# GLU weights requested ahead of the state-space tables, tables requested as buffers come free, decays filled on the spot, input products cut into pieces of 32 states

## The chip, the cores and the metric

The kernel runs on one core of a Trainium2 chip. A core has TensorE (PE, matmul, writes to PSUM), VectorE (DVE), ScalarE (ACT), GpSimd (POOL) and SyncE (SP, which here only queues DMA transfers). Each engine takes its instructions in its own order; between engines there are semaphores. The metric is the device time of one execution in microseconds (us), as the median of several runs.

## The reference

Four pre-norm residual layers over 256 tokens of 1024 features, all in float32. The mixers are stick-breaking attention, a chunked gMLP, a state-space layer ("S5"), and attention again; after each of them comes a convolution-gated MLP ("FFN"). Only the S5 mixer is touched:

```
u  = (xn @ w_in).reshape(B, L, 64 groups, 16)
bu = einsum('gph,blgh->blgp', bbar, u)               # complex, 64 states a group
x_t = a * x_{t-1} + bu_t                             # complex diagonal recurrence
y  = Re(einsum('ghp,blgp->blgh', c, x)) + d_skip * u
a, g = split(gelu(y) @ w_glu);   out = a * sigmoid(g)   # w_glu: 1024 x 2048
```

## The kernel before

**Phases.** The eight phases (attention, FFN, gMLP, FFN, S5, FFN, attention, FFN) run one behind the other, tokens in two blocks of 128. A matmul with weights is three matmuls of split operands: a weight chunk of 128x2048 values is loaded ("raw", 1 MB), and ACT makes its rounded part `wh` (L73) and DVE the rest `wl` (L74), each in two halves of 128x1024.

**One list of weight chunks.** The class `Weights` goes through the chunks of all phases in order. `dma_to(i)` requests raw chunks up to i from SP, `prep_to(i)` converts up to i, `take()` hands out the next. There are three raw buffers and six `wh`/`wl` pairs. S5 has in this list four input chunks (ssin 0 to 3), five tables (gt0, p0, bb, gt1, p1) and eight GLU chunks, called G0 to G7 here. A table is not converted: it is loaded straight into a `wh`/`wl` pair (L56) from DRAM, where GpSimd's DMA queue stored it earlier. gt holds the input matrices, p the output matrices of 16 pairs of groups, bb the input matrices in another layout. `dma_to` stops at a table that has not been reached yet (L35 to L37).

**S5 in the time domain.** 256 tokens are 64 steps of 4. `ucopy(h)` (L1247 on ACT, L1245 on DVE) brings u into place; `gmm(i)` (L1159) makes the input products of a quarter i (8 of 32 pairs of groups) in PSUM, 16 matmuls of a 128x128 weight; each streams 112 columns, of which the following matmul overwrites all but 64. `scan(i)` (L1169 to L1190) rotates the products (four products, a difference on GpSimd, a sum), runs the real recurrence of the two parts (L1178) with the decay table `mg`, and rotates back into the states X(i) with four products on DVE and two sums on GpSimd (L1187, L1190). The rotation factors are the tables t0 (quarter 0) and T (quarters 1 to 3). `kmm(n)` (L1199), `kd(n)` (L1204) and `kevac(n)` (L1211, 16 copies on ACT) make the kernel kk(n) inside a step. `ymm(i, parts)` (L1224) sums the output of quarter i from kk and X in pieces of 32 rows, `yevac(i)` (L1232, L1235, L1236) applies the gelu and splits it, and `glu(c)` multiplies by a chunk of w_glu. `gate` (L1310 to L1312) joins the halves.

**What sets the order.** Nothing is planned at run time: each engine runs in the order of the Python calls, and SP issues transfers in that order, waiting for a buffer where one is not free yet. So a transfer can't pass one that was queued ahead of it. In ACT's and DVE's order the conversion of G0 stands between the first `ucopy` and the second, hence ahead of scan(0). The decay table `mg` is computed by GpSimd during an earlier FFN, stored to DRAM (L1067) and loaded into one of the three raw buffers (L1110), which it holds until scan(3) has read it.

Of the kernel before, what the change touches and what calls it, by code (L numbers as in the profile page):

```python
# [8 lines left out]
F32 = mybir.dt.float32  # L9
# [12 lines left out]
class Weights:  # L22
# [10 lines left out]
    def dma_to(self, i):  # L33
        while self.nd < min(i, len(self.srcs)):
            if self.srcs[self.nd][1] == "tab":  # L35
                if self.npz <= self.nd:
                    return  # L37
                self.nd += 1
                continue
            t = self.raw_p.tile([128, 2048], F32, tag="raw", name=f"raw{self.nd}")  # L40
            for s in (slice(0, 1024), slice(1024, 2048)) if self.nd == 0 else (slice(0, 2048),):
                self.nc.sync.dma_start(t[:, s], self.srcs[self.nd][0][:, s])
            self.raw[self.nd] = t
            self.nd += 1
# [691 lines left out]
class S5(Phase):  # L736
    def __init__(self, k, i, g):
        super().__init__(k, i, g)
        self.done = 0
        d = k.dram  # L740
        self.d_gt = d.tile([128, 2, 2, 2048], F32, name="d_gt")
        self.d_p = d.tile([128, 2, 2, 2048], F32, name="d_p")
        self.d_b = d.tile([128, 2048], F32, name="d_b")
        self.d_w = d.tile([8, 2, 32, 64], F32, name="d_w")
        self.d_t = [d.tile([128, 2048], F32, name=f"t{r}") for r in range(2)]
        self.d_s = d.tile([128, 1024], F32, name="d_s")
        self.d_m = d.tile([128, 2048], F32, name="mg")
        self.par = k.const.tile([128, 19, 32], F32, name="spar")

    def sources(self):  # L750
# [299 lines left out]
    def tables_c(self, pool):  # L1050
        nc = self.nc
        self.own = pool.tile([128, 4], F32, tag="own", bufs=1, name="own")
        nc.sync.dma_start(self.own[:, :], self.k.ins["own"])
        yield from self.tables_t(pool)
        yield from self.tables_p(pool)
        yield from self.tables_m(pool)

    def tables_m(self, pool):
        nc, k = self.nc, self.k
        P = self.par  # L1060
        for h in range(2):
            ps = slice(16 * h, 16 * h + 16)
            m = pool.tile([128, 16, 64], F32, tag="full", bufs=1, name="m")
            nc.gpsimd.tensor_copy(m[:, :, :], P[:, 0, ps].unsqueeze(2).to_broadcast([128, 16, 64]))
            nc.gpsimd.memset(m[:, :, 0:1], 0.0)
            yield
            nc.gpsimd.dma_start(self.d_m[:, 1024 * h:1024 * h + 1024], m[:, :, :].rearrange("p a c -> p (a c)"))  # L1067

    def tables_t(self, pool):

# [33 lines left out]
    def head(self, b, mid):  # L1104
        FFN.head(self, b, mid)
        if b == 0:
            k, w = self.k, self.k.w
            w.prep_to(w.use + 3)
            self.mg = w.raw_p.tile([128, 2048], F32, tag="raw", name="mg")
            self.nc.sync.dma_start(self.mg[:, :], self.d_m[:, :])  # L1110
            self.t0 = k.big.tile([128, D], F32, tag="gb", name="t0")
            for r in range(2):
                self.nc.sync.dma_start(self.t0[:, 512 * r:512 * r + 512], self.d_t[r][:, 0:512])

    def body(self):
        k, nc, w = self.k, self.nc, self.k.w
# [3 lines left out]
        for m in range(3):  # L1120
            FFN.transposes(self, m, k.bank(4 + m))
        k.proj_feat(n, k.bank(7), 1)
        tabs = [w.take() for _ in range(3)]
        TT = []
        for i, tag in enumerate(("xth", "xtl")):
            t = k.big.tile([128, 2048], F32, tag=tag, name=f"T{i}")
            TT.append(t)

        def load_t(c):
            for i in range(2):  # L1130
                nc.sync.dma_start(TT[i][:, c], self.d_t[i][:, c.start + 512:c.stop + 512])

        load_t(slice(0, 512))
        tabs += [w.take() for _ in range(2)]
        load_t(slice(512, 1536))
        gt0, p0, bb, gt1, p1 = (w.hl[t] for t in tabs)
        self.kk.append(bb[1][:, :].rearrange("p (a j c) -> p a j c", a=16, j=4))
        nc.gpsimd.memset(bb[1][:, :], 0.0)
# [4 lines left out]
        MG = self.mg[:, :].rearrange("p (a c) -> p a c", a=32)  # L1143
# [6 lines left out]
        def wide(flat, o, a):  # L1150
            return flat[:, o:min(o + 112, flat.shape[1], o + 512 - 64 * a)]

        def gmm(i):
            for a in range(8):
                pr = 8 * i + a
                u = wide(U[pr // 16].rearrange("p a c -> p (a c)"), 64 * (pr % 16), a)
                for r in range(2):
                    o = gb(i, r)[:, 64 * a:64 * a + u.shape[1]]
                    nc.tensor.matmul(o, GT[r][pr // 16][:, pr % 16, :], u, start=True, stop=True, skip_group_check=True)  # L1159

        def scan(i, mid=lambda: None):
            ps = slice(8 * i, 8 * i + 8)
# [6 lines left out]
            V(out=A(0), in0=b[0], in1=T[0], op=mul)  # L1169
            V(out=A(1), in0=b[1], in1=T[1], op=mul)  # L1170
            G(out=A(0), in0=A(0), in1=A(1), op=sub)
            V(out=A(2), in0=b[1], in1=T[0], op=mul)
            V(out=A(3), in0=b[0], in1=T[1], op=mul)
            mid()
            V(out=A(2), in0=A(2), in1=A(3), op=add)
            fl = lambda v: v.rearrange("p a c -> p (a c)")
            for s in (2, 0):
                nc.vector.tensor_tensor_scan(fl(A(s + 1)), fl(MG[:, ps]), fl(A(s)), 0.0, mul, add)  # L1178
            x = X[i] = [self.tmp.tile([128, 8, 64], F32, tag=f"x{r}", bufs=2, name=f"x{r}") for r in range(2)]
            lo, hi = slice(0, 63), slice(1, 64)  # L1180
            z = [t[1][:, :, lo], t[3][:, :, lo]]
# [2 lines left out]
                nc.gpsimd.memset(x[r][:, :, 0:1], 0.0)  # L1184
            V(out=t[0][:, :, lo], in0=z[0], in1=tr, op=mul)
            V(out=t[2][:, :, lo], in0=z[1], in1=ti, op=mul)
            G(out=x[0][:, :, hi], in0=t[0][:, :, lo], in1=t[2][:, :, lo], op=add)  # L1187
            V(out=x[1][:, :, hi], in0=z[0], in1=ti, op=mul)
            V(out=t[3][:, :, lo], in0=z[1], in1=tr, op=mul)
            G(out=x[1][:, :, hi], in0=t[3][:, :, lo], in1=x[1][:, :, hi], op=sub)  # L1190
# [63 lines left out]
        w.prep_to(w.use + 1)  # L1254
        ucopy(1, False)
        kmm(0)
        kmm(1)
        gmm(1)

        def lags():  # L1260
            for n in range(2):
                kd(n)
                kevac(n)

        scan(0, lags)
        gmm(2)
        ymm(0, K_)
        scan(1)
        ymm(0, X_)
        yevac(0)  # L1270
        gmm(3)
        ymm(1, K_ + X_)
        scan(2)
        yevac(1)
        ymm(2, K_)
        w.prep_to(w.use + 2)
        scan(3)
        acc = [(k.bank(0), k.bank(1)), (k.bank(3), k.bank(4))]
        self.glu(0, w.take(), acc, (0, 1))
        ymm(2, X_)  # L1280
        yevac(2)
        w.prep_to(w.use + 2)
# [119 lines left out]
```

## Time and profile before

| | |
|---|---|
| median of three runs | 1232.25 us (1228.05 to 1233.34) |
| profiled execution, its own time | 1229.2 us |
| span of its instructions | 1227.4 us, 1.8 us less |
| PE busy, weight loads busy | 97%, 89% of the span |
| DVE, ACT, POOL busy | 73%, 58%, 14% |
| mean granted TensorE clock | 0.987 |
| DMA | 239.54 MB, mean 195 GB/s |

The strips of the page cut the span into 40 slices. PE shows 9 (90% and more) in nearly all of them; the lowest digits apart from the first, 6 and 8, stand in slices 21 and 22, which is where S5's body lies (about 612 to 705 us). The timeline lists instructions in order of time: start, duration, engine, line, operation, output from inputs, tile, and in brackets the idle time of the engine and what ended it. "x64" means that so many records were merged. A matmul on float32 operands that are not split shows two records. The chain of waits follows the end of a stretch back from each instruction to what released it.

### The profile page before, as it was taken

The numbers are of one execution on the slowest core, as the hardware profiler recorded it, in microseconds if no ns is written. First come the engines' busy times: TensorE is split into PE (matmuls) and PEld (weight loads), VectorE is DVE, ScalarE is ACT, GpSimd is POOL, SyncE is SP. The second block draws the span as 40 slices with busy tenths as digits, with TensorE's granted clock in tenths as the row PEclk, the third lists the DMA queues.
The fourth block names the chain that finished last, engine by engine and source line by source line (L and its number), as shares of the span: only waits on it lengthen the run. The fifth ranks groups of instructions, "written<-read, shape, count | busy, mean of one in ns | idle before, by whom it ended". The sixth has DMA issues, their size and how long they took to land.

```text
span 1227.4 us, 21740 instructions
## 1 busy us (share of the span) xinstructions
PE 1191.1 (97%) x8944; PEld 1092.2 (89%) x8944; DVE 893.1 (73%) x1268; ACT 706.4 (58%) x1068; POOL 173.2 (14%) x314
## 2 busy tenths in 40 slices
PE   8999999999999999999968799999999999999997
PEld 5898999999897999998957699999988988999996
DVE  5665599789767699899339858866756665886673
ACT  6665576567554565667336546655545655665551
POOL 3885000000384000001103000000000000000000
PEclk9999999999999999999979899999999999999999
DMA  8533457877655266587571635655445332565530
GB/s 298 214 111 113 174 199 269 272 257 276 220 214 202 111 251 221 211 301 273 224 291 36 253 113 206 241 176 201 172 155 206 128 131 106 200 230 189 206 121 35
DMA packets 49988, 239.54 MB, mean 195 GB/s; under 512 B 14944, under 2 KB 15840, under 8 KB 24544
## 3 DMA queue, kind: packets, MB, share of 16 engines
q1 hardware_dynamic: 46352, 224.78, 50.9%
q0 software_dynamic: 3392, 13.11, 2.7%
q8 instruction: 70, 1.15, 0.4%
q14 instruction: 30, 0.25, 0.1%
q10 hardware_dynamic: 144, 0.26, 0.1%
HBM read 223.84 MB, written 14.29 MB: 194 GB/s over the span
## 4 chain that ended last, share of the span: by engine, by line
PE 89%; DVE 5%; DMA 2%; ACT 2%; issue 1%; SPq 0%; POOL 0%; DVEq 0%; POOLq 0%; ACTq 0%
PE pst L126 15%; PE pst L128 15%; PE pst L127 15%; PE pst L134 13%; PE pst L136 13%; PE pst L135 13%; DMA raw<-in_glu_dram 2%; PE pst L536 1%; DVE wl L74 1%; PE pst L181 1%; PE pst L512 1%; PE pst L553 1%; DVE wl L70 1%; DVE t L1178 1%; DMA x<-in_x_dram 1%
## 5 line engine op out<-in xcount | busy, mean ns | idle before, releaser
L74 DVE TENSOR_TENSOR wl<-raw,wh 128x1024 fp32r<-128x1024 f32 x344 | 417.4, 1238 | 75.8 <-ACT wh L73 75.8
L126 PE MATMUL pst<-xth,wh 128*128 128x256 f32 x1552 | 441.0, 284 | 0.0
L127 PE MATMUL pst<-xtl,wh 128*128 128x256 f32 x1552 | 439.2, 283 | 0.0
L128 PE MATMUL pst<-xth,wl 128*128 128x256 f32 x1552 | 439.1, 283 | 0.0
L73 ACT ACTIVATE wh<-raw 128x1024 fp32r<-128x1024 f32 x344 | 350.5, 1049 | 29.8 <-DMA raw<-in_glu_dram 22.7
L126 PEld LDWEIGHTS pst<-xth,wh 128*128 128x128 f32 x1552 | 297.7, 192 | 2.3
L127 PEld LDWEIGHTS pst<-xtl,wh 128*128 128x128 f32 x1552 | 297.8, 192 | 1.2
L128 PEld LDWEIGHTS pst<-xth,wl 128*128 128x128 f32 x1552 | 297.8, 192 | 0.0
L410 DVE SCALAR_TENSOR_TENSOR y<-pst,cw,y 128x255 f32<-128x255 f32 x352 | 160.7, 479 | 72.8 <-ACT y L406 66.6
L134 PE MATMUL pst<-wh,gh 128*128 128x512 f32 x512 | 202.3, 395 | 5.2 <-DVE gate L1311 2.5
L135 PE MATMUL pst<-wl,gh 128*128 128x512 f32 x512 | 200.5, 392 | 0.0
L136 PE MATMUL pst<-wh,gl 128*128 128x512 f32 x512 | 200.1, 391 | 0.0
L406 ACT ACTIVATE y<-pst,cw 128x256 f32<-128x256 f32 x176 | 88.1, 557 | 69.4 <-PE pst L128 64.8
L134 PEld LDWEIGHTS pst<-wh,gh 128*128 128x128 f32 x512 | 96.8, 189 | 25.6 <-DVE gate L1311 2.9
L136 PEld LDWEIGHTS pst<-wh,gl 128*128 128x128 f32 x512 | 96.6, 189 | 21.0 <-DVE gl L690 0.4
L135 PEld LDWEIGHTS pst<-wl,gh 128*128 128x128 f32 x512 | 96.7, 189 | 18.3
L134 PE MATMUL pst<-wh,xth 128*128 128x256 f32 (+1 forms) x336 | 105.9, 315 | 0.0
L135 PE MATMUL pst<-wl,xth 128*128 128x256 f32 (+1 forms) x336 | 105.4, 314 | 0.1
L136 PE MATMUL pst<-wh,xtl 128*128 128x256 f32 (+1 forms) x336 | 105.4, 314 | 0.1
L165 POOL TENSOR_TENSOR r<-m,mhalf 128x1 f32<-128x1 f32 x20 | 11.1, 554 | 666.4 <-DVE m L163 657.9
L416 ACT ACTIVATE y<-y 128x256 f32<-128x256 f32 x88 | 36.4, 419 | 75.5 <-DVE y L410 75.2
L200 ACT ACTIVATE gh<-y 128x256 fp32r<-128x256 f32 x88 | 36.1, 418 | 75.0 <-DVE y L417 75.0
(180 smaller groups left out, 1240.6 us busy)
## 6 DMA issues: line engine op xcount, KB each, us to landing
raw<-in_up_dram SPq DMA_DIRECT2D x88, 1024.0 KB, 4.9
raw<-in_down_dram SPq DMA_DIRECT2D x44, 1024.0 KB, 4.9
raw<-in_wqk_dram SPq DMA_DIRECT2D x16, 1024.0 KB, 5.0
raw<-in_wo_dram SPq DMA_DIRECT2D x8, 1024.0 KB, 4.8
raw<-in_glu_dram SPq DMA_DIRECT2D x8, 1024.0 KB, 4.9
raw<-in_wv_dram SPq DMA_DIRECT2D x7, 1024.0 KB, 4.9
gb<-in_g_dram SPq DMA_DIRECT2D x9, 512.0 KB, 5.7
d_gt<-gf POOLq DMA_DIRECT2D x4, 1024.0 KB, 7.7
```

What stands on the lines that cost most here:

```text
L73: nc.scalar.activation(h[:, s], r[:, s], AF.Copy)
L74: nc.vector.tensor_tensor(out=l[:, s], in0=r[:, s], in1=h[:, s], op=ALU.subtract)
L126: nc.tensor.matmul(out, h[:, cols], xh, start=first, stop=False, skip_group_check=True)
L127: nc.tensor.matmul(out, h[:, cols], xl, start=False, stop=False, skip_group_check=True)
L128: nc.tensor.matmul(out, l[:, cols], xh, start=False, stop=last, skip_group_check=True)
L134: nc.tensor.matmul(out, ah, h[:, cols], start=first, stop=False, skip_group_check=True)
L135: nc.tensor.matmul(out, ah, l[:, cols], start=False, stop=False, skip_group_check=True)
L136: nc.tensor.matmul(out, al, h[:, cols], start=False, stop=last, skip_group_check=True)
L200: self.nc.scalar.activation(g[0][:, j], src, AF.Copy)
L406: nc.scalar.activation(y[:, cs], p[:, cs], AF.Identity, scale=cw[:, s, m, 2:3], bias=cw[:, s, m, 3:4])
L410: nc.vector.scalar_tensor_tensor(y[:, o + tap:o + 256], p[:, o:o + 256 - tap], cw[:, s, m, 2 - tap:3 - tap], y[:, o + tap:o + 256], ALU.mu ...
L416: nc.scalar.activation(y[:, 256:512], y[:, 256:512], AF.Silu)
```

## The change

1. `dma_to` no longer stops at tables: it skips them. In `head(0)` three GLU chunks G0, G1, G2 are requested in the place where `mg` was.
2. `head(1)` ends with `prep_to(use + 6)`: the tables bb, gt1 and p1 are queued there, each waiting on its own `wh`/`wl` pair, and no longer in `body` behind the first T load.
3. `mg` is no longer computed ahead, stored and loaded. GpSimd fills it in each scan, 128x512 at a time, right behind the difference of the rotation; it has one buffer.
4. `gmm` computes 32 states at a time: four matmuls with a 128x32 weight, each into its own 32 rows of PSUM, where one matmul with a 128x128 weight was, and 64 columns instead of 112.
5. The two sums that end a scan go from GpSimd to DVE.
6. The order in `body`: `kmm(1)` behind gmm(2), `kd(1)` and `kevac(1)` in scan(1), both parts of `ymm(0)` behind scan(1), the conversion of G1 ahead of scan(2) instead of scan(3), and glu(0) ahead of scan(3) in the call order.

```diff
     def dma_to(self, i):
         while self.nd < min(i, len(self.srcs)):
             if self.srcs[self.nd][1] == "tab":
-                if self.npz <= self.nd:
-                    return
                 self.nd += 1
                 continue
...
         yield from self.tables_p(pool)
-        yield from self.tables_m(pool)
-
-    def tables_m(self, pool):
...
     def head(self, b, mid):
...
             w.prep_to(w.use + 3)
-            self.mg = w.raw_p.tile([128, 2048], F32, tag="raw", name="mg")
-            self.nc.sync.dma_start(self.mg[:, :], self.d_m[:, :])
+            w.dma_to(w.use + 9)
             self.t0 = k.big.tile([128, D], F32, tag="gb", name="t0")
             for r in range(2):
                 self.nc.sync.dma_start(self.t0[:, 512 * r:512 * r + 512], self.d_t[r][:, 0:512])
+        else:
+            self.k.w.prep_to(self.k.w.use + 6)
...
-        tabs = [w.take() for _ in range(3)]
+        tabs = [w.take() for _ in range(5)]
...
         def gmm(i):
+
             for a in range(8):
-                pr = 8 * i + a
-                u = wide(U[pr // 16].rearrange("p a c -> p (a c)"), 64 * (pr % 16), a)
+                h, c = (8 * i + a) // 16, (8 * i + a) % 16
                 for r in range(2):
-                    o = gb(i, r)[:, 64 * a:64 * a + u.shape[1]]
-                    nc.tensor.matmul(o, GT[r][pr // 16][:, pr % 16, :], u, start=True, stop=True, skip_group_check=True)
+                    for q in range(4):
+                        nc.tensor.matmul(gb(i, r)[32 * q:32 * q + 32, 64 * a:64 * a + 64],
+                                         GT[r][h][:, c, 32 * q:32 * q + 32], U[h][:, c, :],
+                                         start=True, stop=True, skip_group_check=True)
...
             G(out=A(0), in0=A(0), in1=A(1), op=sub)
+            mg = self.tmp.tile([128, 8, 64], F32, tag="mg", name="mg")
+            nc.gpsimd.tensor_copy(mg[:, :, :], self.par[:, 0, ps].unsqueeze(2).to_broadcast([128, 8, 64]))
+            nc.gpsimd.memset(mg[:, :, 0:1], 0.0)
...
-            G(out=x[0][:, :, hi], in0=t[0][:, :, lo], in1=t[2][:, :, lo], op=add)
+            V(out=x[0][:, :, hi], in0=t[0][:, :, lo], in1=t[2][:, :, lo], op=add)
...
-            G(out=x[1][:, :, hi], in0=t[3][:, :, lo], in1=x[1][:, :, hi], op=sub)
+            V(out=x[1][:, :, hi], in0=t[3][:, :, lo], in1=x[1][:, :, hi], op=sub)
...
         kmm(0)
-        kmm(1)
         gmm(1)
-
-        def lags():
-            for n in range(2):
-                kd(n)
-                kevac(n)
-
-        scan(0, lags)
+        scan(0, lambda: (kd(0), kevac(0)))
         gmm(2)
-        ymm(0, K_)
-        scan(1)
-        ymm(0, X_)
+        kmm(1)
+        scan(1, lambda: (kd(1), kevac(1)))
+        ymm(0, K_ + X_)
         yevac(0)
         gmm(3)
         ymm(1, K_ + X_)
+        w.prep_to(w.use + 2)
         scan(2)
         yevac(1)
         ymm(2, K_)
-        w.prep_to(w.use + 2)
-        scan(3)
         acc = [(k.bank(0), k.bank(1)), (k.bank(3), k.bank(4))]
         self.glu(0, w.take(), acc, (0, 1))
+        scan(3)
```

SP's queue around the tables, before (d_gt, d_p and d_b are the stored tables gt, p and bb; t_88 and t_89 are the two stored rotation tables; `t` is t0):

```order
L56 DMA wl_6302<-d_p 128x2048
L1110 DMA mg<-mg 128x2048
L1113 DMA t_6393<-t_88 128x512
L56 DMA wh_6471<-d_b 128x2048
L1131 DMA T_6534<-t_88 128x512
L56 DMA wh_6538<-d_gt 128x2048
L56 DMA wl_6544<-d_p 128x2048
L1131 DMA T_6534<-t_88 128x1024
L42 DMA raw_6583<-in_glu_dram 128x2048
```

and with the change:

```order
L54 DMA wl_6293<-d_p 128x2048
L40 DMA raw_6382<-in_glu_dram 128x2048
L40 DMA raw_6384<-in_glu_dram 128x2048
L40 DMA raw_6386<-in_glu_dram 128x2048
L1097 DMA t_6388<-t_88 128x512
L54 DMA wh_6466<-d_b 128x2048
L54 DMA wh_6469<-d_gt 128x2048
L54 DMA wl_6475<-d_p 128x2048
L1117 DMA T_6537<-t_88 128x512
L1117 DMA T_6537<-t_88 128x1024
L40 DMA raw_7192<-in_glu_dram 128x2048
```

G0 to G2 moved from behind the last T load to ahead of t0, and gt1 and p1 from behind the first T load to ahead of it. G3 is now the first chunk behind the T loads.

GpSimd in scan(0), before:

```order
L1171 TENSOR_TENSOR t_6691<-t_6691,t_6692 128x512
L1184 MEMSET x_6737 128x8
L1187 TENSOR_TENSOR x_6737<-t_6691,t_6693 128x8x63
L1190 TENSOR_TENSOR x_6738<-t_6694,x_6738 128x8x63
L1171 TENSOR_TENSOR t_6795<-t_6795,t_6796 128x512
```

and with the change:

```order
L1149 TENSOR_TENSOR t_6744<-t_6744,t_6745 128x512
L1151 COPY mg<-spar 128x512
L1152 MEMSET mg 128x8
L1165 MEMSET x_6776 128x8
L1149 TENSOR_TENSOR t_6882<-t_6882,t_6883 128x512
```

The two sums that ended a scan are gone from GpSimd; the fill of `mg` stands behind the difference, and the recurrence on DVE waits for it.

DVE between scan(1) and scan(2), before (the last operation of scan(1), the remainder of the gelu output, the first product of scan(2)):

```order
L1189 TENSOR_TENSOR t_6798<-t_6798,T_6534 128x8x63
L1236 TENSOR_TENSOR gl<-y,gh 128x512
L1169 TENSOR_TENSOR t_6999<-pst,T_6534 128x512
```

and with the change:

```order
L1170 TENSOR_TENSOR t_6885<-t_6885,T_6537 128x8x63
L1171 TENSOR_TENSOR x_6915<-t_6885,x_6915 128x8x63
L1217 TENSOR_TENSOR gl<-y,gh 128x512
L72 TENSOR_TENSOR wl_7187<-raw_6384,wh_7186 128x1024 x2
L1147 TENSOR_TENSOR t_7194<-pst,T_6537 128x512
```

The sum of scan(1) joined DVE's order, and the conversion of G1 moved ahead of scan(2).

More of the change, by code (lines that the diff above doesn't have):

```diff
@@ L746, in __init__ @@
         self.d_s = d.tile([128, 1024], F32, name="d_s")
-        self.d_m = d.tile([128, 2048], F32, name="mg")
         self.par = k.const.tile([128, 19, 32], F32, name="spar")
@@ L1055, in tables_c @@
         yield from self.tables_p(pool)
-        yield from self.tables_m(pool)
-    def tables_m(self, pool):
[L1059 to L1067, printed above, removed]
     def tables_t(self, pool):
@@ L1127, in body @@
             TT.append(t)
-        def load_t(c):
+        for c in (slice(0, 512), slice(512, 1536)):
             for i in range(2):
                 nc.sync.dma_start(TT[i][:, c], self.d_t[i][:, c.start + 512:c.stop + 512])
-        load_t(slice(0, 512))
-        tabs += [w.take() for _ in range(2)]
-        load_t(slice(512, 1536))
         gt0, p0, bb, gt1, p1 = (w.hl[t] for t in tabs)
@@ L1142, in body @@
         BB = [bb[0][:, 1024 * r:1024 * r + 1024].rearrange("p (a c) -> p a c", a=32) for r in range(2)]
-        MG = self.mg[:, :].rearrange("p (a c) -> p a c", a=32)
         add, sub, mul = ALU.add, ALU.subtract, ALU.mult
@@ L1146, in body @@
         gb = lambda i, r: k.bank(((0, 1), (2, 5), (0, 1), (2, 7))[i][r])
-        def wide(flat, o, a):
-            return flat[:, o:min(o + 112, flat.shape[1], o + 512 - 64 * a)]
         def gmm(i):
             for a in range(8):
-                pr = 8 * i + a
-                u = wide(U[pr // 16].rearrange("p a c -> p (a c)"), 64 * (pr % 16), a)
+                h, c = (8 * i + a) // 16, (8 * i + a) % 16
                 for r in range(2):
-                    o = gb(i, r)[:, 64 * a:64 * a + u.shape[1]]
-                    nc.tensor.matmul(o, GT[r][pr // 16][:, pr % 16, :], u, start=True, stop=True, skip_group_check=True)
+                    for q in range(4):
+                        nc.tensor.matmul(gb(i, r)[32 * q:32 * q + 32, 64 * a:64 * a + 64],
+                                         GT[r][h][:, c, 32 * q:32 * q + 32], U[h][:, c, :],
+                                         start=True, stop=True, skip_group_check=True)
         def scan(i, mid=lambda: None):
@@ L1177, in scan @@
             for s in (2, 0):
-                nc.vector.tensor_tensor_scan(fl(A(s + 1)), fl(MG[:, ps]), fl(A(s)), 0.0, mul, add)
+                nc.vector.tensor_tensor_scan(fl(A(s + 1)), fl(mg[:, :, :]), fl(A(s)), 0.0, mul, add)
             x = X[i] = [self.tmp.tile([128, 8, 64], F32, tag=f"x{r}", bufs=2, name=f"x{r}") for r in range(2)]
@@ L1256, in body @@
         kmm(0)
+        gmm(1)
+        scan(0, lambda: (kd(0), kevac(0)))
+        gmm(2)
         kmm(1)
-        gmm(1)
-        def lags():
-            for n in range(2):
-                kd(n)
-                kevac(n)
-        scan(0, lags)
-        gmm(2)
-        ymm(0, K_)
-        scan(1)
-        ymm(0, X_)
+        scan(1, lambda: (kd(1), kevac(1)))
+        ymm(0, K_ + X_)
         yevac(0)
```

## The prediction

> **What bounds the kernel now.** TensorE is busy nearly everywhere, so I looked first for the place where it is not. The two low slices point to S5's body, and the windows over it show how much is open there (columns: window, length, busy time of PE, its weight loads, DVE, ACT and POOL, granted clock, DMA share, GB/s):
>
> ```profile
> 584.00:612.00 28.00, 28.00 (x228) 27.52 (x227) 10.31 (x15) 10.26 (x19) 4.81 (x4) 1.00 0.63 245
> 612.00:636.00 24.00, 15.41 (x198) 13.74 (x196) 4.34 (x9) 4.30 (x9) 0.00 (x0) 0.86 0.82 328
> 636.00:682.00 46.00, 35.24 (x820) 30.50 (x824) 43.14 (x53) 28.12 (x56) 16.87 (x20) 0.88 0.20 71
> ```
>
> From 612 to 636 us DVE and ACT work 4.3 us of 24 while DMA is loaded; from 636 to 682 DVE works 43 of 46 us and DMA hardly. So the stage waits for data first and then for DVE's scans. The chain of waits from 612 to 705 us names the data:
>
> ```profile
> 612.65 0.32 SPq L1131
> ...
> 616.74 16.34 DMA raw<-in_glu_dram
> ```
>
> At 612.65 the last projection has released the space of the T tables, and SP goes on; at 616.74 it gets to G0, behind all tables, and G0 takes 16.34 us to land. Its conversion stands in ACT's and DVE's order ahead of everything in the scans. The timeline of DVE shows the price (scan(0) is 636.64 to 645.98, scan(1) to 655.15):
>
> ```profile
> 614.51 1.75 DVE L1245 COPY U<-pst 32x256 f32<-32x256 f32 x4 [1.60 <-ACT U L1247]
> 634.25 2.36 DVE L74 TENSOR_TENSOR wl<-raw,wh 128x1024 fp32r<-128x1024 f32 x2 [17.99 <-ACT wh L73]
> 636.64 0.69 DVE L1169 TENSOR_TENSOR t<-pst,t 128x512 f32<-128x512 f32 x1
> ...
> 643.72 0.68 DVE L1188 TENSOR_TENSOR x<-t,t 128x504 f32<-128x504 f32 x1
> 644.31 1.74 DVE L1189 TENSOR_TENSOR t<-t,t 128x504 f32<-128x504 f32 x1
> 645.98 0.68 DVE L1169 TENSOR_TENSOR t<-pst,T 128x512 f32<-128x512 f32 x1
> ...
> 648.48 0.73 DVE L1175 TENSOR_TENSOR t<-t,t 128x512 f32<-128x512 f32 x1
> 649.25 2.34 DVE L1178 TENSOR_TENSOR_SCAN t<-mg,t 128x512 f32<-128x512 f32 x2
> ...
> 653.41 1.74 DVE L1189 TENSOR_TENSOR t<-t,T 128x504 f32<-128x504 f32 x1
> ...
> 658.21 0.68 DVE L1169 TENSOR_TENSOR t<-pst,T 128x512 f32<-128x512 f32 x1
> ...
> 671.10 0.68 DVE L1169 TENSOR_TENSOR t<-pst,T 128x512 f32<-128x512 f32 x1
> ```
>
> PE had the input products of scan(0) ready at 620.7:
>
> ```profile
> 620.33 0.39 PE L1159 MATMUL pst<-U,wl 128*128 128x64 f32 x2
> ```
>
> and ACT had been free since 614.5, with a long row of copies and the first gelu of the output queued behind the conversion:
>
> ```profile
> 612.93 1.54 ACT L1247 ACTIVATE U<-pst 32x256 f32<-32x256 f32 x4 [1.78 <-DVE U L1245]
> 633.16 2.00 ACT L73 ACTIVATE wh<-raw 128x1024 fp32r<-128x1024 f32 x2 [18.69 <-DMA raw<-in_glu_dram]
> 635.19 6.20 ACT L1247 ACTIVATE U<-pst 32x256 f32<-32x256 f32 x16
> 641.41 7.22 ACT L1211 ACTIVATE kk<-pst 32x512 f32<-32x512 f32 x16
> 648.66 7.04 ACT L1211 ACTIVATE wl<-pst 32x512 f32<-32x512 f32 x16
> 655.72 1.19 ACT L1232 ACTIVATE y<-pst 128x512 f32<-128x512 f32 x1
> 656.94 0.63 ACT L1235 ACTIVATE gh<-y 128x512 fp32r<-128x512 f32 x1
> ```
>
> **G0 in time.** SP issued the first table at 583.85, `mg` at 588.35 and bb at 599.83:
>
> ```profile
> 583.85 0.34 SPq L56 DMA_DIRECT2D wh<-d_gt  x1
> ...
> 588.35 0.39 SPq L1110 DMA_DIRECT2D mg<-mg  x1
> ...
> 599.83 0.32 SPq L56 DMA_DIRECT2D wh<-d_b  x1
> ```
>
> The body's first projection follows the head's last matmul at 605.40, and a window in which DMA is full moves 419 GB/s:
>
> ```profile
> 605.40 0.28 PE L126 MATMUL pst<-xth,wh 128*128 128x256 f32 x1
> ```
>
> ```profile
> 620.00:630.00 10.00, 5.89 (x135) 4.94 (x134) 0.00 (x0) 0.00 (x0) 0.00 (x0) 0.83 1.02 419
> ```
>
> G0 takes mg's place. From 583.85 to the end of G2 there are seven transfers of 1 MB; at 419 GB/s (the saturated window) that is 17.5 us, so all three are there by 602. G2 must wait for the third buffer; behind it t0 and bb wait in SP's queue, and bb is not issued before 599.83 anyway. gt1 waits for the pairs that the head's last weights leave, at the latest 605.4, and p1 after it. Everything from 583.85 to p1 is 12.5 MB, 13.1 million bytes, 31.3 us at 419 GB/s: p1 lands at 615.2 at the earliest.
>
> Now ACT converts G0 at 614.47 (2.00 us), DVE from 616.26 (end of its copies) for 2.36 us, to 618.6. For gmm(0), the pieces of 32 states have a near relative in the trace, ymm, with the same 128x32 weight and 64 columns:
>
> ```profile
> 654.86 1.10 PE L1224 MATMUL pst<-U,kk 128*32 128x64 f32 x64
> 655.78 1.08 PE L1224 MATMUL pst<-x,wh 128*32 128x64 f32 x64
> ...
> 681.90 1.94 PE L1224 MATMUL pst<-x,wl 128*32 128x64 f32 x64 [0.99 <-POOL x L1190]
> ```
>
> 64 records follow each other in 0.92 us at the full clock, 14.4 ns each, and in some 1.87 us at the halved one. After the last copy of u, 40 pieces (80 records) remain of gmm(0): 1.15 to 2.35 us, the upper value at the halved clock, as PE has just idled. Both paths meet at 618.7. **Scan(0) starts at 618.7 instead of 636.64: 17.9 us gained.** Behind it PE needs 1.85 us each for kmm(0) (64 records of 128 columns, twice ymm's) and gmm(1) (128 records of 64); both run beside scan(0) and aren't waited for before scan(1).
>
> **The scan itself.** Before, a scan held DVE for 9.2 to 9.3 us, and scan(3) had its last state at 681.85, 10.75 us after its start, because GpSimd ended it:
>
> ```profile
> 643.95 1.56 POOL L1187 TENSOR_TENSOR x<-t,t 128x504 f32<-128x504 f32 x1 [4.58 <-DVE t L1186]
> ...
> 647.40 1.27 POOL L1171 TENSOR_TENSOR t<-t,t 128x512 f32<-128x512 f32 x1 [0.18 <-DVE t L1170]
> ...
> 680.38 1.47 POOL L1190 TENSOR_TENSOR x<-t,x 128x504 f32<-128x504 f32 x1 [0.62 <-DVE t L1189]
> ```
>
> The old fill of the decays is the row of line 1064 (shortest, middle and longest in ns, for 1024 columns):
>
> ```profile
> L1064 POOL COPY m<-spar x2: 1238/1420/1602, 554.2 to 560.3; 128x1024 f32<-128x1024 f32 x2
> ```
>
> L1189 takes 1.74 us while L1187 runs on GpSimd, its twin L1188 0.68: two operands in SBUF on DVE wait for GpSimd. So the two sums cost DVE 0.6 each but take this 1.06 us of waiting away: a tail of six operations, 3.7 us with two dependent steps. The fill costs at the front. GpSimd ends its difference 2.7 us after a scan's start (647.40 + 1.27 against 645.98), then copies 128x512, half of the L1064 row, 0.6 to 0.8 us. Meanwhile L1175, a sum of two SBUF operands, is ready at 2.5. If the copy passes beside it, only the recurrence waits, to 3.7 after the start (3.27 before); if one of them holds up the other, to 4.2. I take the second, since L1175 is of L1189's kind: 4.15 + 2.35 + 3.7 = **10.2 us a scan**. Bounds: 9.7 with the copy beside it, 11.0 if the copy is stretched as L1187 is, to 1.56.
>
> The Trainium skill (SBUF — State Buffer, Who interferes with whom) says that a DVE instruction with two SBUF inputs contends with a GpSimd one that reads SBUF, and that the loser waits for all of it. By that rule the copy, which reads the decays from SBUF, would block the sum, which gives the 10.2; the 1.74 of L1189 agrees, but no row here shows it for a copy. Without the rule it would be 9.7, 2 us less over four scans.
>
> **From scan to scan.** scan(0) 618.7 to 628.9; scan(1) to 639.1. ACT: second ucopy from 616.5 to 622.7, kevac(0) to 629.9, kevac(1) behind kd(1), which DVE reaches 2.7 us into scan(1), 631.6 to 638.6, y and gh of quarter 0 to 640.5, G1's rounding to 642.5. DVE: remainder of quarter 0 at 641.1, G1's rest to 643.9, scan(2) to 654.1, remainder, scan(3) 654.7 to 664.9. On PE, glu(0) waits until scan(2) has read its two banks, at 646.3, and then has 7.8 us before X(2); PE had 10 us to spare in this stage (35 of 46 busy in the second long window). In terms of the old row starts: scans 0 and 1 cost 20.4 instead of 18.5 (+1.9); from there to scan(2) 4.8 instead of 3.06 (+1.7, the moved conversion of G1); scan(2) up to scan(3) 10.8 instead of 12.9 (-2.1); scan(3) 10.2 instead of 10.75 (-0.55).
>
> **After the last state.** The chain there is unchanged in kind:
>
> ```profile
> 691.29 6.04 DMA raw<-in_glu_dram
> ...
> 702.05 0.50 PE pst L134
> ```
>
> G7 can be requested only when G4's conversion leaves its raw buffer, and the gate stands behind G7's conversion: 20.2 us from X(3) to 702.05. The early chunks don't change this, since G5 to G7 wait for buffers that are freed behind scan(3) in both. I deduct 0.45, half of what ymm loses at the halved clock.
>
> **Sum:** -17.9 + 1.9 + 1.7 - 2.1 - 0.55 - 0.45 = **-17.4 us**. The removed fills, stores and load of mg lie beside PE work that has no gap (28.00 of 28 us in the first window) and count nothing; as GpSimd's queue loses work there, no cost can arise either. Against the profiled execution's 1229.2 this gives 1211.8, against the median 1232.25 it gives 1214.9. The four times known average 1230.7; I predict **1213.5 us**. Four scans at 9.7 or at 11.0 move it by -2.0 or +3.2, the end behind X(3) by 0.45 either way: a gain of 13.7 to 19.9 us, 1208 to 1220 with the 2.6 us by which the known times lie around their mean.
>
> **Rivals.**
> *p1 takes G0's place.* kmm(1) (1.85 us) must be done when scan(1) reaches kd(1) at 631.6, so p1 must be there by 629.75; behind kd(1) stands the rest of scan(1) and all later work of DVE. At 419 GB/s it has 14 us to spare; it decides below 13.1 million bytes in 46 us, 285 GB/s. At the 245 of the first window p1 lands at 637.4, 7.6 us late: about 1221. For it: the request queue is long. Against: 245 was a window with too little to load.
> *The fill drags the scans.* If GpSimd's copy and DVE obstruct each other beyond the bound, say 12 us a scan, four scans lose 7 us: about 1220.
> *Nothing gained.* G0 is not there, because its raw buffer or its place among the pairs comes free late. The pair is ssin 3's, free after the last projection at 612.65, in time; the time would be about 1230.
> *Slower: the pieces run one after another.* In ymm the four pieces of a group have different moving operands; in gmm they share one. If they did not overlap, each record would take 106 to 110 ns (its weight load) or 219 (its matmul). From the last u, PE has 80 + 3 x 128 records of gmm and 6.5 us of kmm and ymm(0) ahead of scan(3), so X(3) comes at 633.0 us plus the time of 464 records; from 105 ns each this passes the old 681.85. At 219 ns it is 734.6, 53 us later: 1283. Here are the rows:
>
> ```profile
> L1224 PEld LDWEIGHTS pst<-x,wh 128*32 128x32 f32 x256 | 3.9, 110 | 4.1 <-POOL x L1187 4.1
> L1224 PE MATMUL pst<-x,wh 128*32 128x64 f32 x256 | 4.4, 220 | 3.3 <-POOL x L1187 3.3
> ```
>
> Against it: ymm's 14.4 ns, although all its pieces have weights and outputs of the same form.
>
> **How the numbers follow.** Forecast 0.75; p1 late 0.08; dragging fill 0.07; gain above 21 us 0.03; nothing gained 0.04; slower 0.03. A measurement of this kernel can tell about 0.5%, 6 us, from no change. The first four are faster by more than that in nearly all of their width: faster 0.92, same 0.05, slower 0.03. The range takes in the forecast's 1208 to 1220, the two rivals above it to their middle, and 2 us below for the larger gain: 1206 to 1221.
>
> **What would show it.** G0's conversion on ACT directly behind the first copies, near 614.5, with no wait for DMA; the first product of scan(0) near 618.7; the recurrence 3.7 to 4.2 us after a scan's start; no scan row of 1.74 us; 128 gmm records in about 1.9 us; the last state near 665 and the matmul that waits for the gate near 684. The prediction is wrong if DVE waits inside a scan for kd(1), if a scan takes over 11 us, or if the chain's end behind X(3) grows beyond 20 us because the GLU chunks come late.

## The result and the profile after

The changed kernel takes 1214.14 us (median of 4 runs, 1213.76 to 1214.6) against 1232.3 us beside it: a ratio of 0.9859, 95% interval 0.9836 to 0.9883. Its profiled execution took 1214.6 us (span 1212.8), the one of before 1229.2. The ratios here and below leave out single disturbed executions far longer than the others of their kernel (2946.64 us of one kernel below, 1278.08 of another).

The windows of the prediction's first fence, now over the changed kernel (window, length, busy time of PE, its weight loads, DVE, ACT and POOL, granted clock, DMA share, GB/s):

```profile
584.00:612.00 28.00, 28.00 (x226) 27.46 (x225) 9.54 (x13) 10.26 (x19) 5.37 (x4) 1.00 0.95 381
612.00:636.00 24.00, 12.95 (x636) 11.71 (x638) 21.13 (x33) 19.53 (x44) 4.02 (x10) 1.00 0.54 216
636.00:682.00 46.00, 38.09 (x902) 31.51 (x893) 38.67 (x48) 23.26 (x32) 5.00 (x10) 1.00 0.33 118
```

The data that loaded DMA at 0.82 between 612 and 636 us now passes in good part before 612, at 0.95 instead of 0.63. DVE works 21 of the 24 us that it had waited through, and GpSimd has 5 us of work left in the long window instead of 17. The requests on SP show how:

```profile
584.25 0.34 SPq L54 DMA_DIRECT2D wh<-d_gt  x1
...
588.75 6.00 SPq L40 DMA_DIRECT2D raw<-in_glu_dram  x3
...
606.37 0.42 SPq L54 DMA_DIRECT2D wl<-d_p  x1
...
613.06 1.75 SPq L1117 DMA_DIRECT2D T<-t  x4
```

G0 to G2 are asked for 4.5 us behind the first table, p1's second half at 606.37; it lands 13.9 us later, at 620.3. DVE's timeline from there on:

```profile
614.90 1.75 DVE L1226 COPY U<-pst 32x256 f32<-32x256 f32 x4 [1.60 <-ACT U L1228]
616.69 2.36 DVE L72 TENSOR_TENSOR wl<-raw,wh 128x1024 fp32r<-128x1024 f32 x2
619.08 0.69 DVE L1147 TENSOR_TENSOR t<-pst,t 128x512 f32<-128x512 f32 x1
...
621.68 1.14 DVE L1156 TENSOR_TENSOR t<-t,t 128x512 f32<-128x512 f32 x1
622.92 2.34 DVE L1159 TENSOR_TENSOR_SCAN t<-mg,t 128x512 f32<-128x512 f32 x2
...
629.11 0.68 DVE L1147 TENSOR_TENSOR t<-pst,T 128x512 f32<-128x512 f32 x1
...
632.37 0.30 DVE L1185 TENSOR_TENSOR pst<-pst,di 128x128 f32<-128x128 f32 x1 [0.78 <-PE pst L1180]
...
644.87 0.68 DVE L1147 TENSOR_TENSOR t<-pst,T 128x512 f32<-128x512 f32 x1
...
647.38 0.69 DVE L1156 TENSOR_TENSOR t<-t,t 128x512 f32<-128x512 f32 x1
648.75 2.34 DVE L1159 TENSOR_TENSOR_SCAN t<-mg,t 128x512 f32<-128x512 f32 x2 [0.68 <-POOL x L1165]
...
655.62 0.68 DVE L1147 TENSOR_TENSOR t<-pst,T 128x512 f32<-128x512 f32 x1
...
665.16 0.68 DVE L1171 TENSOR_TENSOR x<-t,x 128x504 f32<-128x504 f32 x1
```

The conversion at 616.69 waits for nothing, and scan(0) follows it; the four scans start at 619.08, 629.11, 644.87 and 655.62. Whole runs are shifted against each other by up to 3 us in front of this stage, so from here on times are counted from the first table's request (583.85 before, 584.25 after), and the prediction's own times likewise:

| us behind the first table's request | before | predicted | after |
|---|---|---|---|
| scan(0) starts | 52.79 | 34.85 | 34.83 |
| scan(1) starts | 62.13 | 45.05 | 44.86 |
| scan(2) starts | 74.36 | 60.05 | 60.62 |
| scan(3) starts | 87.25 | 70.85 | 71.37 |
| last state | 98.00 | 81.05 | 81.59 |
| matmul that waits for the gate | 118.20 | 100.80 | 101.52 |
| gate of the second half | 129.41 | not predicted | 114.32 |

The stage gains 16.7 us up to the gate's matmul, and 15.1 us one step later: 1.6 us are lost behind the gate.

Two things in the trace were not foreseen. The first is in the chain of waits, from 620 us on:

```profile
619.78 0.65 PE pst L1135 x42
620.43 3.13 issue
623.57 1.99 PE pst L1135 x127
625.55 1.90 issue
627.45 1.38 PE pst L1135 x84
628.88 1.10 PE pst L1180 x40
629.98 1.47 issue
```

TensorE runs 127 or 124 records and then stands still with nothing that the profile shows as a releaser. Four more such pauses follow, at 635.81, 639.91, 643.91 and 647.58: seven in all, 4.0 us from one to the next ((647.58 - 623.57) / 6), 14.3 us together. gmm(1), gmm(2) and kmm(1), 5.5 us by the rows of the prediction, last from 619.78 to 632.3, 12.5 us. The second is behind the last state:

```profile
674.55 6.51 DMA raw<-in_glu_dram
...
683.10 0.49 ACT L1284
...
685.02 0.70 DVE gate L1285
685.77 0.50 PE pst L132
```

```profile
685.77 0.50 PE L132 MATMUL pst<-wh,gh 128*128 128x512 f32 x1 [4.46 <-DVE gate L1285]
```

TensorE waits 4.46 us for the gate (2.52 before), and then its granted clock falls: it is 0.50 from 686.6 to 690.0. Here the 5 us behind the gate's matmul in the changed kernel, and below them those of before:

```profile
685.00:690.00 5.00, 4.23 (x12) 3.34 (x13) 4.91 (x7) 4.87 (x7) 0.00 (x0) 0.66 0.91 320
```

```profile
702.00:707.00 5.00, 4.95 (x22) 4.11 (x23) 4.94 (x6) 4.27 (x6) 0.00 (x0) 1.00 0.79 311
```

Over these 5 us the granted clock is 0.66 instead of 1.00, with 12 matmul records instead of 22.

### The profile page after: what moved, and what is told of

It reads as the page before. It is cut to its first block, busy times and chain, and to the rows that moved or that the text cites. A ratio compares the mean times of both kernels' runs of the same rounds, so it can differ in the third digit from the quotient of the medians.

```text
span 1212.8 us, 22510 instructions
## 1 busy us (share of the span) xinstructions
PE 1175.3 (97%) x9328; PEld 1078.3 (89%) x9328; DVE 891.9 (74%) x1276; ACT 705.7 (58%) x1068; POOL 162.2 (13%) x308
## 4 chain that ended last, share of the span: by engine, by line
PE 91%; DVE 4%; ACT 2%; issue 1%; DMA 1%; POOL 0%; DVEq 0%; SPq 0%; POOLq 0%; ACTq 0%
PE pst L124 15%; PE pst L126 15%; PE pst L125 15%; PE pst L132 13%; PE pst L133 13%; PE pst L134 13%; PE pst L534 1%; PE pst L179 1%; DVE wl L72 1%; PE pst L510 1%; PE pst L551 1%; DVE wl L68 1%; ACT wl L1192 1%; DMA raw<-in_glu_dram 1%; DMA gb<-in_g_dram 1%
```

## The experiments

The theory was that the gain hangs on G0's early request, that each scan pays the fill's contention, and that TensorE's pauses come from the supply of its instructions: the change makes 768 more of them. The rivals were p1's transfer, the pieces as the source of the gain, and pauses by accident. Unless said otherwise each kernel is the changed one with the edit shown; the ratios are to the kernel before, run beside it.

**The changed kernel again**, as the yardstick of that chip.

> The changed kernel itself, as the yardstick of this chip: about 1214 us, scan(0) from 619.1, scan(2) from 644.9, the gate's matmul at 685.8. In its profile TensorE should again stand still inside gmm with nothing that releases it, at steps of about 4 us from 623 on; if these pauses were an accident of one execution, they are gone here.

1214.79 us, ratio 0.9847 (0.983 to 0.9864). scan(0) at 34.83 again, the gate's matmul at 100.65, the gate of the second half at 114.22. The pauses are back in the same places of the program (they end at 623.58, 627.19, 630.65, 634.73, 638.56, 642.56 and 646.22 us), with other lengths: 2.83, 1.62, 0.92, 1.78, 1.83, 2.01 and 1.67 us. So they are no accident of one execution. kd(1) did not wait this time, which is why scan(2) is at 59.79 here and at 60.62 above.

**The wide form of the input products.**

```diff
-                for r in range(2):
-                    for q in range(4):
-                        nc.tensor.matmul(gb(i, r)[32 * q:32 * q + 32, 64 * a:64 * a + 64],
-                                         GT[r][h][:, c, 32 * q:32 * q + 32], U[h][:, c, :], ...)
+                flat = U[h].rearrange("p a c -> p (a c)")
+                u = flat[:, 64 * c:min(64 * c + 112, 1024, 64 * c + 512 - 64 * a)]
+                for r in range(2):
+                    nc.tensor.matmul(gb(i, r)[:, 64 * a:64 * a + u.shape[1]], GT[r][h][:, c, :], u, ...)
```

> Only the input products go back to 128-state weights with 112 columns (16 matmuls a group instead of 64); the rest as changed. Theory (TensorE is supplied with instructions in blocks of about 256, one block per 4 us, so the short pieces run at 14 ns inside a block but at 31 ns over many of them): the pauses in gmm go, a group takes 3.6 us as before the change, scan(0) starts 1 to 2 us later because more of gmm(0) is left behind the last copy of u, kd(1) no longer waits (the 2.4 us that the first copies of kevac(1) wait are gone). Both cancel: within 2 us of the changed kernel, 1212.5 to 1216. Rival (the short pieces are what brings the gain, by half of TensorE's time): scan(0) and scan(2) 3 us later or more, 1218.

1216.37 us, ratio 0.9856 (0.9838 to 0.9874). scan(0) starts at 36.80, 1.97 us later, waiting 2.00 us for TensorE, and the gate's matmul is 1.96 later. gmm has none of the pauses left: the 0.38 us of "issue" at its start stands in the kernel before too. Three are left in ymm, whose pieces are unchanged (1.83, 0.92 and 0.58 us). So the pieces are worth about 2 us by the trace; the times can't tell it (the intervals overlap).

**G0 in turn behind the tables.**

```diff
-            w.dma_to(w.use + 9)
```

> G0 to G2 are not asked for past the tables any more, but in turn behind them; the rest as changed. Theory (this line is what scan(0)'s start hangs on): G0 is asked for when the T loads have passed, at 614.8, and is there 5 to 8 us later at some 410 GB/s, so its rounding on ScalarE ends at 622 to 625 and scan(0) starts 624 to 627.5 instead of 619.1: 1219 to 1222. Rival (the earlier start comes from the tables alone, which no longer hold G0 back as long): no change, 1214.

1223.47 us, ratio 0.9922 (0.9905 to 0.9938), apart from the changed kernel's interval. The row of ScalarE's conversion of G0:

```profile
625.09 2.00 ACT L71 ACTIVATE wh<-raw 128x1024 fp32r<-128x1024 f32 x2 [10.28 <-DMA raw<-in_glu_dram]
```

ScalarE waits 10.28 us for the transfer, scan(0) starts at 44.38, 9.55 later. That is more than the 5 to 8 us expected, since p1, which lands at 616.8, and the T loads still fill the DMA engines in front of G0. The rest of the way to the 52.79 of before, 8.4 us, is what the other edits give without it. By the rows G0 is asked for 2.3 us earlier than before (30.6 us behind the first table's request instead of 32.9) and lands 6.1 us faster (10.23 us instead of 16.34); gt1 and p1 are asked for from 603.1 to 606.3 here, and before from 613.5 to 614.9, right ahead of it. No run takes that edit back with G0 late, so its share of the 8.4 us is read from these rows and not measured alone.

**Two tables later.**

```diff
-        tabs = [w.take() for _ in range(5)]
+        tabs = [w.take() for _ in range(3)]
...
+            if c.start == 0:
+                tabs += [w.take() for _ in range(2)]
```

The lines in the head that prepare these tables earlier are left out with it; the two are taken behind the first part of T.

> Three tables are asked for in front of the T loads and gt1 and p1 behind the first half of T, so that p1 comes later; G0 stays early. Theory (p1 has time to spare; what delayed kd(1) in the changed kernel was TensorE's own pauses): p1 lands at about 624.5, ahead of kmm(1), and the time stays, 1213.5 to 1215. Rival p1 (kd(1) waits for the table): DVE waits longer than 0.8 us in scan(1) for the product of line 1180, and the time grows by that, 1217 or more.

1217.04 us, ratio 0.987 (0.9853 to 0.9887). p1's second half is asked for at 617.89 and lands 13.4 us later, at 631.3, not 624.5 as expected. TensorE, and behind it DVE:

```profile
632.18 0.26 PE L1135 MATMUL pst<-U,wl 128*32 128x64 f32 x4 [4.09 <-issue]
```

```profile
637.33 0.30 DVE L1185 TENSOR_TENSOR pst<-pst,di 128x128 f32<-128x128 f32 x1 [3.15 <-PE pst L1180]
```

kd(1) waits 3.15 us, and the gate's matmul comes 3.06 later than in the changed kernel (103.71). By its sign this is the rival's outcome, but the trace does not show p1 as what TensorE waited for: p1 was there 2.1 us before kmm(1) began at 633.41. Two other things held TensorE back. One is the pause inside gmm(2), 4.09 us where the changed kernel has 1.62 at the same record; DMA moved 407 GB/s through it. The other came behind it: the granted clock is 0.50 from 633.3 to 636.7, and kmm(1) takes 3.9 us (kmm(0) in the changed kernel: 1.75). With a pause of 1.62 kmm(1) would have met p1 at 631.3; at the full clock, and with a pause of 0.92 as in the changed kernel's second run, it would have been done near 634.0, while DVE reached kd(1) at 634.2. That is an estimate from these rows. By it p1's arrival alone would have cost nothing, and what later tables cost is the load that they put on DMA during the pause.

How much that load lengthens a pause in general stays open. The first pause, always under load, took 1.12 to 3.98 us in the runs that have it, but it ended 38.6 to 39.3 us behind the first table's request in all of them. It was short (1.12 to 1.46) where the granted clock had been 0.50 for 3.4 us ahead of it, so that TensorE came to it later.

**Pieces of 64 states.**

```diff
-                    for q in range(4):
-                        nc.tensor.matmul(gb(i, r)[32 * q:32 * q + 32, ...], GT[r][h][:, c, 32 * q:32 * q + 32], ...)
+                    for q in range(2):
+                        nc.tensor.matmul(gb(i, r)[64 * q:64 * q + 64, ...], GT[r][h][:, c, 64 * q:64 * q + 64], ...)
```

> The input products in pieces of 64 states: 32 matmuls a group, half of the changed kernel's instructions and twice those of the wide form. Theory (TensorE's instructions come through the DMA queue of kind instruction, 16 KB or 256 of them a packet; the change added 768 instructions and 3 packets, 70 to 73, and the wide form is back at 70): 512 instructions fewer than in the changed kernel, so that queue shows 71 packets; the pauses between 620 and 640 become fewer. Two pieces side by side instead of four: a record takes about 28 ns, 64 records a group 1.8 us, so scan(0) starts within 0.5 us of 619.4 and the time is 1213.5 to 1215.5. Rival (the pauses hang on something else than the number of instructions): packets and pauses as in the changed kernel.

1213.49 us, ratio 0.985 (0.983 to 0.9869). The page's rows of instructions and the DMA queue of kind instruction (packets, MB, share), of before, of the changed kernel, and of this one:

```profile
PE 1191.1 (97%) x8944; PEld 1092.2 (89%) x8944; DVE 893.1 (73%) x1268; ACT 706.4 (58%) x1068; POOL 173.2 (14%) x314
...
q8 instruction: 70, 1.15, 0.4%
```

```profile
PE 1175.3 (97%) x9328; PEld 1078.3 (89%) x9328; DVE 891.9 (74%) x1276; ACT 705.7 (58%) x1068; POOL 162.2 (13%) x308
...
q8 instruction: 73, 1.20, 0.4%
```

```profile
PE 1180.7 (97%) x9072; PEld 1080.6 (89%) x9072; DVE 892.0 (74%) x1276; ACT 706.0 (58%) x1068; POOL 162.5 (13%) x308
...
q8 instruction: 71, 1.16, 0.4%
```

A matmul record and a weight load are one instruction each. 2 x 8944 / 256 = 69.9, 2 x 9328 / 256 = 72.9, 2 x 9072 / 256 = 70.9: the packets are TensorE's instructions, 256 to a packet of 16.4 KB (1.20 MB / 73). The wide form shows 70. The packets' times in the trace tie them to the pauses. Each of the changed kernel's seven pauses ends 1.2 to 1.5 us behind the end of a packet of this queue, the first at 623.57 behind one that ran from 621.19 to 622.28. The same holds, within 1.1 to 1.6 us, for every pause of TensorE over 0.5 us with no releaser between 614 and 662 us in the other traces used here, that of the kernel before included, which has one in ymm (0.95 us). The long pause of the run above fits: its packet starts at 629.60, 3.5 us behind the end of the pause before it, with DMA at 421 GB/s; in the changed kernel's second run it is 1.1 us (624.72 behind 623.58).

Between 620 and 640 us there is one pause of over 0.5 us left (1.24, at 633.51) where the changed kernel has five; scan(0) starts at 34.82, scan(2) at 59.75. So half the instructions do the same.

**Each input product twice** (the second into the same place, so the outcome is the same).

```diff
-                for r in range(2):
+                for r in (0, 1, 0, 1):
```

> Each input product is worked out twice into the same place (the outcome is the same), so gmm has 1024 instructions more. Theory of the instruction supply: the queue of kind instruction shows 77 packets instead of 73, and TensorE needs some 3.7 us for each packet, far over the 14.4 ns a record: in all 10 to 15 us more on its way to kmm(1) and the output products, kd(1) in scan(1) waits for it for 5 us or more, and the time is 1222 to 1230. Rival (the records cost what they show, 512 x 14.4 ns = 7.4 us, beside 10 us to spare): 1215 to 1217.

1228.55 us, ratio 0.9972 (0.996 to 0.9984): 14 us above the changed kernel.

```profile
PE 1187.1 (97%) x9840; PEld 1088.4 (89%) x9840; DVE 891.3 (73%) x1276; ACT 705.9 (58%) x1068; POOL 161.7 (13%) x308
...
q8 instruction: 77, 1.26, 0.4%
```

```profile
642.43 0.30 DVE L1185 TENSOR_TENSOR pst<-pst,di 128x128 f32<-128x128 f32 x1 [5.24 <-PE pst L1180]
```

77 packets as expected; scan(0) starts at 39.34, 4.5 us later, kd(1) waits 5.24, the gate's matmul comes at 115.03, 14.4 later. 1024 instructions cost 14 us, 3.5 us a packet, in a stage where 7.4 us of records at 14.4 ns would have found room. The rival that a record costs what it shows is out. The granted clock was 0.50 from 621.6 to 628.4, but the two packets there took 3.9 us each, against 3.5 to 4.0 behind them, so the lower clock explains little of the 14 us.

**The fill ahead of a scan's products.**

```diff
+            mg = self.tmp.tile([128, 8, 64], F32, tag="mg", name="mg")
+            nc.gpsimd.tensor_copy(mg[:, :, :], self.par[:, 0, ps]...)
+            nc.gpsimd.memset(mg[:, :, 0:1], 0.0)
             V(out=A(0), in0=b[0], in1=T[0], op=mul)
             V(out=A(1), in0=b[1], in1=T[1], op=mul)
             G(out=A(0), in0=A(0), in1=A(1), op=sub)
-            mg = ...                               # the same three lines
```

> GpSimd fills the decays ahead of a scan's first products instead of behind its difference. Theory (the fill holds up the recurrence by its place, 3.84 us instead of 3.27 behind a scan's start): the recurrence starts 3.2 to 3.3 us behind the start of each scan, where the tail of the scan before does not meet the copy; up to 0.6 us a scan, 1.2 to 2 us in all: 1212.5 to 1213.5. Rival: the copy falls into the tail of the scan before, holds up one of its sums and takes the gain back: no change.

1215.47 us, ratio 0.9859 (0.9836 to 0.9882). It ran again for its trace.

> The kernel with GpSimd's fill ahead of a scan's first products once more, for its trace: the one profiled execution of it was a disturbed one of 2945 us, while its other five times lay with the changed kernel's. Theory: the recurrence starts 3.3 us behind the start of the scans, since the copy is over before the products; but the sums of line 1168 or 1171 in the scan before now show a copy's contention (over 1 us instead of 0.68), which takes half or more of it back: gate's matmul 99 to 100.5 us behind the first table's request (100.65 in the changed kernel of that chip), a time that can't be told from 1214.8. Rival: 2 us and more gained, 1212.5.

1214.91 us, ratio 0.9861 (0.9844 to 0.9879). The recurrence starts 3.47, 3.30 and 3.30 us behind the start of scans 0, 2 and 3 (3.84, 3.88 and 3.88 with the fill behind the difference; in scan(1) kd(1) waited). GpSimd's copy for the next scan, and DVE's product beside it:

```profile
650.69 1.12 POOL L1148 COPY mg<-spar 128x512 f32<-128x512 f32 x1 [2.98 <-DVE t L1159]
```

```profile
651.27 1.09 DVE L1167 TENSOR_TENSOR t<-t,T 128x504 f32<-128x504 f32 x1
```

The copy has one buffer and so waits for the recurrence to end; it then meets the tail's products, and one of them takes 1.09 instead of 0.68. Of 0.58 us, 0.41 goes back; from scan(2) to scan(3) it is 10.58 instead of 10.74. The gate's matmul comes at 100.53 (100.65 without this edit). So the 1.2 to 2 us of the first expectation did not come. Its rival was right, and so was the theory of the second expectation: no gain that a time can show.

**The sums back on GpSimd.**

```diff
-            V(out=x[0][:, :, hi], in0=t[0]...
+            G(out=x[0][:, :, hi], in0=t[0]...
-            V(out=x[1][:, :, hi], in0=t[3]...
+            G(out=x[1][:, :, hi], in0=t[3]...
```

> The two sums at a scan's end go back from DVE to GpSimd, the rest as changed. Theory (they cost DVE 0.6 each but take 1.06 of waiting away, and the last scan no longer ends on GpSimd): DVE's rows of 1.74 us return, scans 0 to 2 get no longer or shorter by up to 0.3 us each, the last state comes 1 to 1.5 us later behind scan(3)'s start: 1215 to 1216.5. Rival (DVE is what the stage waits for, so that two operations more on it cost 1.2 us a scan): 1211.

1216.36 us, ratio 0.9875 (0.9857 to 0.9893). DVE's long rows are back, and GpSimd ends the last scan:

```profile
662.71 1.76 DVE L1170 TENSOR_TENSOR t<-t,T 128x504 f32<-128x504 f32 x1
```

```profile
664.55 1.47 POOL L1171 TENSOR_TENSOR x<-t,x 128x504 f32<-128x504 f32 x1 [0.62 <-DVE t L1170]
```

scan(0) to scan(1) is 9.69 instead of 10.03, and the last state is there 11.4 us behind scan(3)'s start (654.62 to 666.02) instead of 10.2. The gate's matmul comes at 101.56, 0.9 later. So the sums on DVE cost 0.3 us in a scan that another follows, and are worth 1.2 in the last one: 0.9 at the gate.

**kevac(1) ahead of scan(1).**

```diff
         scan(0, lambda: (kd(0), kevac(0)))
-        gmm(2)
         kmm(1)
-        scan(1, lambda: (kd(1), kevac(1)))
+        kd(1)
+        kevac(1)
+        gmm(2)
+        scan(1)
```

> kmm(1) in front of gmm(2), and kd(1) and kevac(1) in front of scan(1) instead of inside it. Theory (ScalarE's 16 copies of kevac(1) stand on the path from scan(1) to scan(2), since y(0), its rounding and G1's conversion are queued behind them): kevac(1) follows kevac(0) without the 1.5 us that it waits in the changed kernel, scan(2) starts 1.5 us earlier, the time is about 1213. If only DVE's scans set the pace there, scan(2) stays where it is and the time too.

1215.89 us, ratio 0.9862 (0.9841 to 0.9883). scan(2) starts at 58.32, 1.47 us earlier, and the gate's matmul at 99.43, 1.2 earlier; at the second half's gate 0.8 is left (113.45), and the times can't tell it. So ScalarE's row of copies is on the path between scan(1) and scan(2), as the prediction had it.

**The gates ahead of the conversion.**

```diff
             self.glu(i, w.take(), acc, (0, 1))
-            w.step()
+            if i == 2:
+                w.step()
         for b in range(2):
             self.gate(b, acc[b], k.x[:, b, 0:512])
+        w.step()
```

> The two gates in front of the conversion of the GLU chunk that they stand behind in the changed kernel. Theory (TensorE's 4.4 us of standing still in front of the second half, and the half clock for some 3 us behind it, come from that conversion, which waits for its transfer): the wait falls to about 1.7 us, the clock behind it stays nearer to full, 2.7 to 4.4 us gained: 1210 to 1212. Rival (the GLU chunks' transfers set the end of this stage wherever the gate stands): TensorE waits later for the chunk, and the time stays within 1 us.

1209.7 us, ratio 0.982 (0.9799 to 0.9842). The gate's matmul, and then the 20 us from 680 in the changed kernel (its second run, gate's matmul at 685.23) and here:

```profile
683.94 0.50 PE L132 MATMUL pst<-wh,gh 128*128 128x512 f32 x1 [0.72 <-DVE gate L1287]
```

```profile
680.00:700.00 20.00, 15.57 (x59) 12.32 (x58) 10.44 (x12) 9.36 (x12) 0.00 (x0) 0.83 0.69 261
```

```profile
680.00:700.00 20.00, 19.28 (x86) 15.63 (x85) 14.67 (x17) 13.37 (x18) 0.55 (x1) 1.00 0.80 313
```

TensorE waits 0.72 us instead of 4.43, and its clock stays at 1.00: with the short wait the fall of the clock is gone too. (In the second run of the changed kernel it is 0.50 from 683.4 to 690.3, so it falls within the wait, and 2.4 us are lost behind the gate instead of 1.6.) The gate's matmul gains 3.7 us (96.95), the gate of the second half 6.1 (108.16). From the one to the other it is 11.2 us, as before the change.

**All together**: 64 states, the fill ahead, kevac(1) early, the gates ahead.

> The changed kernel with pieces of 64 states, the fill ahead of a scan's products, kevac(1) ahead of scan(1) and the gates ahead of the last conversion. Worked out from the runs of each alone, in the distance from the first table's request to the second gate (114.2 in the changed kernel of that chip, 108.2 with the gates first, 113.5 with kevac(1) early, 113.5 with 64 states): about 107 us, so 7 us less than the changed kernel and 1206.5 to 1208.5. If the GLU chunks' transfers now set the end of the stage, the gain of the gates alone remains, 1209.5.

1206.3 us, ratio 0.979 (0.9772 to 0.9808), below the changed kernel's interval: 8 us less. The chain ends at

```profile
678.62 0.50 PE pst L132
```

94.57 behind the first table's request, and the gate of the second half is at 105.78.

## Why the prediction was right

**G0 in time: right, to 0.02 us.** The forecast start of scan(0) was ACT's and DVE's order behind the first copies; G0 was there, and the last 40 pieces took 1.14 us (616.71 to 617.85), the lower of the two values given. Taking the early request away costs 9.55 us of the 18; the 8.4 that remain without it go, by the rows above, with the tables' earlier requests. p1 landed at 620.3, which, counted from the first table's request, is 4.7 us behind the earliest that the prediction gave; of its 14 us to spare some 10 were left.

**The scan: right, on the mechanism chosen.** A scan took 10.03 us (forecast 10.2). The recurrence began 3.84 to 3.88 us behind a scan's start where kd(1) did not delay it. That lies between the two values given, 3.7 for a copy that passes beside the sum and 4.2 for one that does not, so the time alone would not decide; the rows do. Copy and sum hold each other up, either way round. In scan(0) the copy is first, and in scan(2) the sum:

```profile
621.66 0.61 POOL L1151 COPY mg<-spar 128x512 f32<-128x512 f32 x1
...
647.45 1.10 POOL L1151 COPY mg<-spar 128x512 f32<-128x512 f32 x1
```

The sum takes 1.14 where the copy takes 0.61, and 0.69 where the copy takes 1.10. The Trainium skill (SBUF — State Buffer, Who interferes with whom) has the one that issues first keep the shared ports and the other wait; both orders of it stand in these rows.

**From scan to scan: right in sum.** scan(1) to scan(2) was forecast at 15.0; it took 15.76 and, in the second run, 14.93. The difference is the wait for kd(1). That wait inside scan(1) was named as what would prove the prediction wrong, and it did occur, 0.78 us. Its place was the p1 rival's, its cause was not: p1 was there at 620.3, more than 8 us before kmm(1). The step that failed is "PE needs 1.85 us each for kmm(0) and gmm(1)": kmm(0) took 1.75, but gmm(1) some 5.2, of which 3.13 are the first pause, and kmm(1), put at 1.85 too, took 3.5 with its pause. The 14.4 ns a record came from a row of 64 records, too few to show a pause, and was carried over to hundreds. It cost little only since a scan of 10 us covers the four-odd us that 256 instructions take; with twice the input products it cost 14 us.

**Behind the last state: right up to the gate, wrong behind it.** From the last state to the gate's matmul it was 19.9 us (19.75 forecast, 20.2 before). But the sum ended there as if nothing could change behind it, and TensorE lost 1.6 us at the lower clock (2.4 in the second run). TensorE came to the wait 15.5 us behind the last state instead of 17.7; before, its granted clock had been 0.50 from 681.0 to 687.8, and here it was 1.00, which is at least a part of the 2.2 us. The gate's matmul came 19.9 us behind the last state instead of 20.2, so the wait grew from 2.52 to 4.46. With the gates first, wait and loss both went. The strip of the kernel before gave a hint that was passed over: PE shows a 7 in slice 23 (675 to 706 us) too, which holds this wait.

**The sum.** Forecast -17.4; the trace shows -16.7 up to the gate and -15.1 behind it, the two profiled executions 14.6, the medians 18.2. So the traces show 0.7 to 2.8 us less than forecast. That 1214.14 came within 1 us of the 1213.5 predicted is in part luck: the profiled execution of before lay 3 us under its median, and no row shown here explains these 3 us. The removed load, fills and stores cost nothing, as forecast: PE is busy 39.00 of 39 us from 545 and 28.00 of 28 us from 584 in both. The order of the calls (item 6) was not taken back as a whole; its rows are scan(2) to scan(3), 10.75 us instead of 12.89 (forecast 10.8). The rivals "fill drags the scans", "nothing gained" and "pieces run one after another" are refuted by the rows above.

## What to carry to other kernels

Follow the stage that waits with DMA full back to the request that stands last in its queue, and move that. When an instruction is split into smaller ones, count the instructions as well as their durations, and take the price from a row of several hundred; here 64-state pieces gave the same time with half as many. Where a chain is shortened on one side, look at which engine now waits longer, and bring what it waits for ahead of work that nobody waits for.

## What the runs showed of the hardware

TensorE's instructions arrive through a DMA queue, 256 to a packet, and where the matmuls are short that supply sets the pace: 4.0 us a packet here, 3.8 in the second run, about 15 ns an instruction or 30 ns a record, against 14.4 ns a record inside a packet. A pause ended 1.1 to 1.6 us behind the end of a packet. With DMA nearly idle pauses were up to 2.1 us long, under load up to 4.1. The Trainium skill (Runtime: NRT & Kernel Launch, Instruction fetch mechanics) gives the block of 256 instructions, which the four packet counts agree with, and calls its cost mostly hidden; these traces show it in the open, the measurement with each product done twice at 3.5 us a packet.

Behind a wait of 4.46 us TensorE's granted clock fell (0.66 over the next 5 us); behind waits of 0.72 and 2.52 us it stayed at 1.00.
